# Hybrid encoder trunk, one core: sums of squares with tokens on partitions, and the condition ahead of the squares

## The chip, the cores and the metric

One Trainium2 chip; the kernel runs on one core. The metric is the device time of one execution in microseconds, 2192.99 us before the change: the median of three runs, 2190.62 to 2194.06. Everything is float32; large matmuls take their operands as pairs of rounded parts, hi and lo, and run three products.

## The reference

Two layers over 256 tokens of width 2048. Each layer is modulated by a condition vector and has two groups of attention heads side by side, then an MLP with squared ReLU:

```
cond = silu(c)
for l in range(2):
    mod = cond @ w_ada[l] + b_ada[l]            # six vectors of 2048
    h = rmsnorm(x) * (1 + sc_a) + sh_a
    proj = h @ w_in[l]                          # dq, dk, dv, cq, ckv, kr
    out_a = diff_attention(dq, dk, dv, positions, bias_table, lam)
    q = rmsnorm(cq, q_norm_g[l]) @ w_uq[l]
    kv = rmsnorm(ckv, kv_norm_g[l]) @ w_ukv[l]
    out_b = mla_attention(q, kv, rope(kr))
    x = x + g_a * (concat(out_a, out_b) @ w_o[l])
    h = rmsnorm(x) * (1 + sc_m) + sh_m
    x = x + g_m * (square(relu(h @ w_mlp_in[l])) @ w_mlp_out[l])
return rmsnorm(x, final_norm_g)
```

where `rmsnorm(x) = x * rsqrt(mean(x*x, -1) + 1e-6) * g`. The change concerns `cond` and all these norms but the last.

## The kernel before

The residual `x` is kept transposed: features on the 128 partitions, 16 blocks of 256 tokens in the free dimension. A norm therefore needs sums across partitions. It squares `x` on ScalarE, adds blocks on VectorE where it can, and multiplies by a 128x128 matrix of constants 1/n (`mean`) on TensorE (`rstd`, L536). Each column of the product is one token's mean, repeated on all 128 partitions. `root` (L542, L543) takes the square root on ScalarE and the reciprocal on VectorE, both of 128x256. The result `rstd` multiplies rows of `x` directly, in `modulated` (`ht`, L620), `latent` (`lt`, L645) and `scaled` (L610).

There are eight such norms: the first, in `setup`, directly over `x`; in each layer the two latent norms (`ckv`, then `cq`); that of layer 0's MLP; and those behind `ahead_rest`, for layer 1's input and layer 1's MLP, where the matmuls start on unnormalised `x` and the norm comes in later. The final norm has its own code and is not touched.

The modulation vectors are products of `cond` with 1 MB tiles of `w_ada`, on VectorE: one instruction of 128x2048 per tile (`ada`, L304), whose sum is one column of `macc`. `cond` is made in `setup`: one row of 2048 is multiplied by a row of `mean` in four `pc` matmuls (L357), which spreads it over 128 partitions, and ScalarE applies Silu (L358). Between two parts of layer 0's input projection (`by_k`, `pk`), four tiles are summed for the next two blocks of `x`; the first `ht` needs four. SyncE issues nearly all loads in program order. The tiles of `w_ada` and the split weights share five buffers (`raw`), so a load waits until VectorE has released the buffer it takes.

The instruction order on each engine is set by a scheduler that goes through the program in the order written, and by manual constraints (`follow`: the one instruction is issued behind the other, without a wait). Other small work lies between the parts of the first projection (`fills`): the relative bias, `lambdas` (`pl`, a matmul of 4 columns), the rope tables. `setup`, `bias_setup` and `distances` prepare that from `pos`, `K` (constants) and `vec` (small parameters).

Of the kernel before, what the change touches and what calls it, by code (L numbers as in the profile page):

```python
# [10 lines left out]
F32 = mybir.dt.float32  # L11
F32R = mybir.dt.float32r
I32 = mybir.dt.int32
AF = mybir.ActivationFunctionType
# [3 lines left out]
P = 128  # L18
T = 256
TX = T + 2  # L20
D = 2048
NK = D // P
# [5 lines left out]
EPS = 1e-6  # L28
# [75 lines left out]
class Trunk:  # L104
# [230 lines left out]
    def setup(self):  # L335
        nc, io, cp = self.nc, self.io, self.cp
        self.ada_plan()
        self.cond = cp.tile([P, D], F32, name="cond")
        row = self.wp.tile([1, D], F32, tag="raw", name="c_row", bufs=5)
        nc.sync.dma_start(row, io["c"])  # L340
        self.pos = cp.tile([P, T + 8], I32, name="pos")
        nc.scalar.dma_start(self.pos, io["pos"])
        self.K = cp.tile([P, NCONST], F32, name="K")
        nc.scalar.dma_start(self.K, io["consts"])
        self.vec = cp.tile([P, NVEC], F32, name="vec")
        nc.scalar.dma_start(self.vec, io["vec"])
        self.x = cp.tile([P, NK, T], F32, name="x")
        for q in range(4):
            nc.sync.dma_start(self.x[:, 4 * q : 4 * q + 4], io["xT"][:, 4 * q : 4 * q + 4])
        self.mean = {}  # L350
        for n in (D, 2 * P):
            self.mean[n] = cp.tile([P, P], F32, name=f"mean{n}")
            nc.gpsimd.memset(self.mean[n], 1.0 / n)
        for j in range(4):
            c = slice(512 * j, 512 * j + 512)
            ps = self.bank("pc").rearrange("p a b -> p (a b)")
            nc.tensor.matmul(ps, self.mean[D][:1], row[:, c], start=True, stop=True)  # L357
            nc.scalar.activation(self.cond[:, c], ps, AF.Silu, scale=float(D))  # L358
        self.eps = cp.tile([P, 1], F32, name="eps")
        nc.gpsimd.memset(self.eps, EPS)  # L360
        self.ident = cp.tile([P, P], F32, name="ident")
        make_identity(nc, self.ident)
        self.bias_setup()
        self.rel = {0: self.distances(0)}
        ps = self.bank("pn")[:, 0]
        for k in range(0, NK, 2):
            t = self.t("sqx")
            last = nc.scalar.activation(t, self.x[:, k : k + 2], AF.Square)
            for i in range(2):
                nc.tensor.matmul(ps, self.mean[D], t[:, i], start=k + i == 0, stop=k + i == NK - 1)  # L370
        self.follow(nc.scalar.activation(self.s("warm", 1), self.eps, AF.Sqrt), last)
        return self.root(ps)

    def fills(self):
        m = {"l": self.lambdas, "r": self.rope_setup, "e": lambda: self.bias_out(self.last)}
# [23 lines left out]
    def bias_setup(self):  # L399
        nc, K, pos = self.nc, self.K, self.pos  # L400
        n = T + 8
        half = lambda s, dt=F32: self.up.tile([P, 2 * T], dt, tag="u", name=self.name(s))
        ih, il, fh, fl = (half(s, dt)[:, :n] for s, dt in (("ih", I32), ("il", I32), ("fh", F32), ("fl", F32)))
        nc.vector.tensor_scalar(ih, pos, 16, None, ALU.arith_shift_right)
        nc.vector.tensor_scalar(il, pos, 0xFFFF, None, ALU.bitwise_and)
        nc.vector.tensor_copy(fh, ih)
        nc.vector.tensor_copy(fl, il)
        lh, ll = [], []
        for i in range(2):
            lsc = half("lsc")  # L410
            trep = self.vec[:, V_T + 16 * i : V_T + 16 * i + 16].unsqueeze(2).broadcast_to([P, 16, 32])
            delta = K[:, C_DELTA : C_DELTA + 32].unsqueeze(1).broadcast_to([P, 16, 32])
            nc.vector.tensor_tensor(lsc.rearrange("p (a b) -> p a b", a=16), trep, delta, ALU.mult)
            lh.append(half("lsch", F32R))
            ll.append(half("lscl", F32R))
            nc.scalar.activation(lh[i], lsc, AF.Copy)
            nc.vector.tensor_tensor(ll[i], lsc, lh[i].bitcast(F32), ALU.subtract)
        self.bias = self.cp.tile([P, HD, 2, T], F32, name="bias")
        self.bt = fh, fl, lh, ll
# [109 lines left out]

    def rstd(self, acc, n):  # L530

        nc = self.nc
        ps = self.bank("pn")[:, 0]
        acc = acc[:2] + acc[3:]
        for i, a in enumerate(acc):
            nc.tensor.matmul(ps, self.mean[n], a, start=i == 0, stop=i == len(acc) - 1)  # L536
        return self.root(ps)

    def root(self, ps):
        nc = self.nc  # L540
        r = self.cp.tile([P, T], F32, tag="rstd", name=self.name("rstd"), bufs=2)
        nc.scalar.activation(r, ps, AF.Sqrt, bias=self.eps)  # L542
        nc.vector.reciprocal(r, r)  # L543
        return r

    def ahead(self, l, sh, sc, src):

# [35 lines left out]
    def ahead_rest(self, st, first, acc, after, loads=0):  # L583

        h = []
        for p in range(first, 8):
            if p >= loads:
                self.rate = RATE_K
            if p == after:
                r = self.rstd(acc, D)  # L590
            self.ahead_step(st, p)
            if p >= after:
                upto = 2 * (p - after + 1) if loads else NK * (p - after + 1) // (8 - after)
                if p == 7:
                    upto = NK
                while len(h) < upto:
                    h += self.modulated(
                        r, len(h), self.mod[st.l, st.sh], self.mod[st.l, st.sc], after=self.lo if loads else None
                    )
        st.r = r  # L600
        return h
# [28 lines left out]
            self.last = ins  # L630
        return out

    def latent(self, vals, g):

        nc = self.nc
        acc = None
        for v in vals:
            acc = self.sumsq(acc, v, scale=2.0 if len(vals) == 2 else 1.0)
        r = self.rstd(acc, D if len(vals) == 2 else 2 * P)
        out = []  # L640
        for b, v in enumerate(vals):
            t = self.t("lt")
            for i in range(2):
                k = 2 * b + i
                nc.vector.scalar_tensor_tensor(t[:, i], v[:, i], g[:, k : k + 1], r, ALU.mult, ALU.mult)  # L645
            out += self.split(t, "lat")
        return out
# [25 lines left out]
    def layer(self, l, acc, st):  # L673
# [34 lines left out]
        def keys():  # L708
            ps = self.bank("pkr")
            self.tile_cols(ps[:, 0], io["w_kr"][l], h)  # L710
            self.kr = self.rope_k(ps[:, 0])
# [38 lines left out]
        def probs(hd):  # L750
            return lambda: a.append(self.diff_probs(l, self.diff_scores(hd, q[hd], kk[hd])))
# [13 lines left out]
        if l == 0:  # L765
            next_by_k(range(done, 4))(h)
            q += [self.copy(ps, "q", qs) for ps in banks[3:]]
            ckv += self.latent([ckr], gkv)
            kk.append(self.copy(later[0], "k", -1.0))
            q.append(self.copy(later[1], "q", qs))  # L770
            keys()
            order = [(0, kk, -1.0), (2, kk, -1.0), (4, kk, -1.0)]
            for n, (i, dst, scale) in enumerate(order):
                col(i, dst, scale)()
                if n == 0:
                    cq += self.latent(cqr, gq)
                got = self.diff_scores(n, q[n], kk[n])
                col(i + 1, dst, scale)()
                a.append(self.diff_probs(l, got, self.copied if n == 2 else None))
        else:  # L780
            def two(i, dst, scale):
                ps = self.wides([io["w_q"][0, i + j] for j in range(2)], h)
                dst.append(self.joined(ps, self.u("qk"), scale))

            two(0, q, qs)
            two(8, kk, -1.0)
            ckv += self.latent([ckr], gkv)
            for hd in range(1, HD):
                two(2 * hd, q, qs)
                probs(hd - 1)()  # L790
                two(8 + 2 * hd, kk, -1.0)
                if hd == 1:
                    cq += self.latent(cqr, gq)
            keys()
            self.rate = RATE_A2
        up_k()
# [450 lines left out]
def _layout(i):  # L1247
# [4 lines left out]
    pos = f["positions"][0]  # L1252
    order = [j + 4 * t for j in range(4) for t in range(2)]
    posq = np.tile(pos.reshape(8, 32).T, (4, 1))[:, order]
    a["pos"] = np.ascontiguousarray(np.concatenate([np.broadcast_to(pos, (P, T)), posq], 1))
    a["consts"] = consts()
    feat = lambda v, n: v.reshape(n, P).T
    vec = [feat(f["b_ada"][l], 96) for l in range(2)]
    vec += [feat(f["diff_subln_g"][l], 2) for l in range(2)]
# [1 line left out]
    vec += [feat(f["kv_norm_g"][l], 2) for l in range(2)]  # L1261
    vec += [np.stack([f[f"diff_lambda_{a}{j}"][l] for a in "qk" for l in range(2) for j in (1, 2)], 1)]
    vec += [np.repeat(f["rel_bias_table"].reshape(8, 4, HD).transpose(1, 0, 2).reshape(4, 32), 32, 0)]
    a["vec"] = np.ascontiguousarray(np.concatenate(vec, 1))
    assert a["vec"].shape == (P, NVEC)
    a["fg"] = np.ascontiguousarray(np.broadcast_to(f["final_norm_g"], (P, D)))
    a["w_ada"] = np.ascontiguousarray(f["w_ada"].transpose(0, 2, 1)).reshape(2, 96, P, D)
    keep = {k: [] for k in ("w_a", "w_d", "w_t", "w_a1", "w_q", "w_kr", "w_dv", "w_uq", "w_uk", "w_uv", "w_oa", "w_ob", "w_m0", "w_n0", "w_m1", "w_m2")}
# [49 lines left out]
```

## Time and profile before

| what | value |
|---|---|
| median of three runs | 2192.99 us |
| the profiled execution | 2192.04 us |
| its span, first to last instruction | 2190.2 us |
| mean granted TensorE clock | 0.995 |
| TensorE busy | 2155.7 us, 98% |
| VectorE busy | 1620.7 us, 74% |
| ScalarE busy | 1153.3 us, 53% |
| mean DMA rate | 268 GB/s |

The median of the runs lies 0.95 us above the profiled execution. All rows below come from this one execution. PE is TensorE, PEld its weight load, DVE VectorE, ACT ScalarE, POOL GpSimd, SP SyncE. A matmul's listed duration contains its way through the array; how fast matmuls follow each other is read from their starts.

### The profile page before, as it was taken

Reading aid. Unit: us, or ns where it says so; the run is one execution under the profiler, and the core shown is the slowest. Engines: PE = TensorE matmul, PEld = TensorE weight load, DVE = VectorE, ACT = ScalarE, POOL = GpSimd, SP = SyncE. Lnnn points to the kernel's source line nnn. Section 1 sums busy time; section 2 is a strip of 40 time slices with the busy share of each in tenths; the row PEclk is TensorE's granted clock in tenths of the full one; section 3 lists DMA queues with packets and bytes.
Section 4 is the critical chain, followed back from the end, with each engine's and each line's share of the span. In section 5 each row is a group of like instructions: output and inputs, shape, how many; then the busy total and the mean of one; then the engine's idle time right before and its main releaser. Section 6 shows DMA issues by size and latency. Waiting matters only on the chain.

```text
span 2190.2 us, 30242 instructions
## 1 busy us (share of the span) xinstructions
PE 2155.7 (98%) x11938; PEld 1884.5 (86%) x11938; DVE 1620.7 (74%) x2162; ACT 1153.3 (53%) x1730; POOL 26.7 (1%) x43
## 2 busy tenths in 40 slices
PE   7999999999999999999999999999999999999998
PEld 5899889898888888888888888999888888888886
DVE  7989988988778778788799876798545545545566
ACT  6555664455455355355456555647546535534544
POOL 0000000000000000000001000000000000000000
PEclk9999999999999999999999999999999999999999
DMA  9986888799888888888868765686555555555552
GB/s 400 383 337 233 342 335 298 258 362 346 310 322 323 328 305 339 328 308 318 323 231 307 250 250 211 243 301 217 192 194 187 189 195 189 190 194 191 187 198 94
DMA packets 85826, 586.39 MB, mean 268 GB/s; under 512 B 9522, under 2 KB 9906, under 8 KB 19634
## 3 DMA queue, kind: packets, MB, share of 16 engines
q1 hardware_dynamic: 85106, 583.84, 72.6%
q8 instruction: 93, 1.52, 0.3%
q10 hardware_dynamic: 576, 0.62, 0.1%
q14 instruction: 51, 0.41, 0.0%
HBM read 582.32 MB, written 2.10 MB: 267 GB/s over the span
## 4 chain that ended last, share of the span: by engine, by line
PE 92%; DVE 6%; ACT 2%; DMA 1%; issue 0%; ACTq 0%; DVEq 0%; SPq 0%
PE ps L208 24%; PE ps L211 13%; PE py L1022 11%; PE py L1020 11%; PE py L1024 11%; DVE ada L304 3%; PE pk L189 2%; PE pk L188 2%; PE pk L187 2%; PE pv L258 2%; PE pv L260 2%; PE pv L259 2%; PE pk L244 1%; DVE lo L151 1%; PE pss L189 1%; PE pss L187 1%
## 5 line engine op out<-in xcount | busy, mean ns | idle before, releaser
L151 DVE TENSOR_TENSOR lo<-raw,hi 128x1024 fp32r<-128x1024 f32 (+1 forms) x720 | 849.2, 1195 | 463.5 <-ACT hi L148 294.6
L148 ACT ACTIVATE hi<-raw 128x1024 fp32r<-128x1024 f32 (+1 forms) x720 | 737.6, 1035 | 632.1 <-PE py L1024 360.4
L208 PE MATMUL ps<-h,hi 128*128 128x512 f32 x2016 | 472.1, 391 | 1.2 <-ACT hi L148 1.2
L208 PEld LDWEIGHTS ps<-h,hi 128*128 128x128 f32 x2016 | 374.9, 188 | 77.8 <-ACT hi L148 2.1
L304 DVE SCALAR_TENSOR_TENSOR ada<-ada,cond 128x2048 f32<-128x2048 f32 x192 | 437.4, 2285 | 1.4 <-ACT cond L358 1.1
L1020 PE MATMUL py<-hi,hid 128*128 128x512 f32 x1024 | 326.5, 390 | 0.0
L1022 PE MATMUL py<-lo,hid 128*128 128x512 f32 x1024 | 325.9, 389 | 0.0
L1024 PE MATMUL py<-hi,hid 128*128 128x512 f32 x1024 | 325.7, 389 | 0.0
L211 PEld LDWEIGHTS ps<-h,lo 128*128 128x128 f32 x2016 | 250.5, 192 | 5.0
L211 PE MATMUL ps<-h,lo 128*128 128x256 f32 x2016 | 252.0, 283 | 0.0
L1022 PEld LDWEIGHTS py<-lo,hid 128*128 128x128 f32 x1024 | 192.2, 188 | 40.2 <-DVE lo L151 0.4
L1024 PEld LDWEIGHTS py<-hi,hid 128*128 128x128 f32 x1024 | 192.2, 188 | 40.0
L1020 PEld LDWEIGHTS py<-hi,hid 128*128 128x128 f32 x1024 | 191.3, 188 | 38.8
L1059 ACT ACTIVATE sum<-ps 128x256 f32<-128x256 f32 x110 | 42.1, 383 | 128.3 <-PE ps L211 128.0
L187 PE MATMUL pk<-h,hi 128*128 128x256 f32 x304 | 86.4, 288 | 7.0 <-ACT hi L148 3.6
L189 PE MATMUL pk<-h,lo 128*128 128x256 f32 x304 | 86.7, 289 | 0.8 <-DVE lo L151 0.8
L188 PE MATMUL pk<-h,hi 128*128 128x256 f32 x304 | 87.1, 288 | 0.0
L181 DVE TENSOR_TENSOR hid<-relu,hid 128x256 fp32r<-128x256 f32 x128 | 48.3, 421 | 46.7 <-ACT hid L180 46.7
L244 PE MATMUL pk<-hf,w 128*128 128x256 f32 x288 | 66.1, 391 | 9.4 <-ACT hf L628 9.4
L244 PEld LDWEIGHTS pk<-hf,w 128*128 128x128 f32 x288 | 56.4, 197 | 18.3 <-ACT hf L628 10.1
L187 PEld LDWEIGHTS pk<-h,hi 128*128 128x128 f32 x304 | 58.9, 195 | 8.3 <-ACT hi L148 4.4
L623 ACT ACTIVATE h<-ht,mod 128x256 fp32r<-128x256 f32 x64 | 29.5, 500 | 59.4 <-DVE ht L620 59.2
(262 smaller groups left out, 2590.2 us busy)
## 6 DMA issues: line engine op xcount, KB each, us to landing
raw<-in_w_m SPq DMA_DIRECT2D x238, 1024.0 KB, 4.9
ada<-in_w_ada SPq DMA_DIRECT2D x192, 1024.0 KB, 5.0
raw<-in_w_ob SPq DMA_DIRECT2D x24, 1024.0 KB, 4.8
raw<-in_w_dv SPq DMA_DIRECT2D x16, 1024.0 KB, 5.1
raw<-in_w_q SPq DMA_DIRECT2D x16, 1024.0 KB, 5.5
raw<-in_w_n SPq DMA_DIRECT2D x16, 768.0 KB, 5.6
w<-in_w_a SPq DMA_DIRECT2D x24, 384.0 KB, 9.3
raw<-in_w_a SPq DMA_DIRECT2D x12, 768.0 KB, 6.4
```

What stands on the lines that cost most here:

```text
L148: ins = nc.scalar.activation(hi, v, AF.Copy)
L151: ins = nc.vector.tensor_tensor(lo, v, hi.bitcast(F32), ALU.subtract)
L187: mm(ps, hi, x[0], start=first, stop=False, skip_group_check=shared)
L188: mm(ps, hi, x[1], start=False, stop=False, skip_group_check=shared)
L189: mm(ps, lo, x[0], start=False, stop=last, skip_group_check=shared)
L208: mm(ps.rearrange("p a b -> p (a b)"), part(w, 0, k), both, start=k == 0, stop=False)
L211: mm(ps[:, 0], part(w, 1, k), x, start=False, stop=k == nk - 1)
L244: self.nc.tensor.matmul(ps, w[i][:, j * P : j * P + P], whole[i], start=first, stop=last, skip_group_check=True)
L304: ins = nc.vector.scalar_tensor_tensor(w, w, 1.0, self.cond, ALU.mult, ALU.mult, accum_out=acc[:, i : i + 1])
L1020: mm(o, xh[:, tok], hi[:, part[j]], start=start, stop=False)
L1022: mm(o, xh[:, tok], lo[:, part[j]], start=False, stop=False)
L1024: mm(o, xl[:, tok], hi[:, part[j]], start=False, stop=stop)
```

## The change

Each mean of squares is now computed with tokens on partitions. `sums` makes the square the loaded operand, 128 features x 128 tokens, and streams one column of `mean`, so that each 128 tokens give one column of the result. `root` then works on 128x2. `spread` turns the two columns back to rows: a column of `r`, repeated 128 times, is transposed by TensorE into the other half of the same PSUM bank, and ScalarE copies it to `rstd`. The latent norms and those of `ahead_rest` put other work between the two halves, `total` and `spread`.

In `setup` three loads (`pos`, `consts`, `vec`) become one (`tab`), a Silu of one column is issued first on ScalarE, and the squares and the Copy of `bias_setup` are constrained to stand behind the Silu of `cond`.

```diff
-        self.pos = cp.tile([P, T + 8], I32, name="pos")
-        nc.scalar.dma_start(self.pos, io["pos"])
-        self.K = cp.tile([P, NCONST], F32, name="K")
-        nc.scalar.dma_start(self.K, io["consts"])
-        self.vec = cp.tile([P, NVEC], F32, name="vec")
-        nc.scalar.dma_start(self.vec, io["vec"])
+        tab = cp.tile([P, T + 8 + NCONST + NVEC], F32, name="tab")
+        nc.scalar.dma_start(tab, io["tab"])
+        self.pos = tab[:, : T + 8].bitcast(I32)
+        self.K = tab[:, T + 8 : T + 8 + NCONST]
+        self.vec = tab[:, T + 8 + NCONST :]
...
+        self.lead = nc.scalar.activation(self.s("warm", 1), self.eps, AF.Silu)
+        leads = []
         for j in range(4):
             c = slice(512 * j, 512 * j + 512)
             ps = self.bank("pc").rearrange("p a b -> p (a b)")
             nc.tensor.matmul(ps, self.mean[D][:1], row[:, c], start=True, stop=True)
-            nc.scalar.activation(self.cond[:, c], ps, AF.Silu, scale=float(D))
...
-        self.bias_setup()
+            self.lead = nc.scalar.activation(self.cond[:, c], ps, AF.Silu, scale=float(D))
+            leads.append(self.lead)
+            if j == 0:
+                self.bias_setup()
         self.rel = {0: self.distances(0)}
-        ps = self.bank("pn")[:, 0]
+        ps = self.bank("pn")
         for k in range(0, NK, 2):
             t = self.t("sqx")
             last = nc.scalar.activation(t, self.x[:, k : k + 2], AF.Square)
+            self.follow(last, leads[min(3, 1 + k // 4)])
             for i in range(2):
-                nc.tensor.matmul(ps, self.mean[D], t[:, i], start=k + i == 0, stop=k + i == NK - 1)
+                self.sums(ps, t[:, i], D, k + i == 0, k + i == NK - 1)
         self.follow(nc.scalar.activation(self.s("warm", 1), self.eps, AF.Sqrt), last)
-        return self.root(ps)
+        return self.spread(*self.root(ps))
...
     def rstd(self, acc, n):
+        return self.spread(*self.total(acc, n))
...
+    def sums(self, ps, a, n, first, last):
+        for t in range(2):
+            self.nc.tensor.matmul(
+                ps[:, 0, t : t + 1], a[:, t * P : (t + 1) * P], self.mean[n][:, :1],
+                start=first and t == 0, stop=last, skip_group_check=True,
+            )
+
     def root(self, ps):
         nc = self.nc
-        r = self.cp.tile([P, T], F32, tag="rstd", name=self.name("rstd"), bufs=2)
-        nc.scalar.activation(r, ps, AF.Sqrt, bias=self.eps)
+        r = self.s("root")
+        nc.scalar.activation(r, ps[:, 0, :2], AF.Sqrt, bias=self.eps)
         nc.vector.reciprocal(r, r)
-        return r
+        return ps, r
+
+    def spread(self, ps, r):
+        for t in range(2):
+            self.nc.tensor.transpose(
+                ps[:, 1, t * P : (t + 1) * P], r[:, t : t + 1].broadcast_to([P, P]), self.ident
+            )
+        out = self.cp.tile([P, T], F32, tag="rstd", name=self.name("rstd"), bufs=2)
+        self.nc.scalar.activation(out, ps[:, 1], AF.Copy)
+        return out
```

VectorE, from the end of its setup work to the first `ht`. `macc` and `mod` are the sums and vectors of the modulation, `rel` belongs to the bias. Before:

```order
L432 TENSOR_SCALAR rel_161<-rel_161 128x512
L304 SCALAR_TENSOR_TENSOR ada_213,macc_80<-ada_213,cond 128x2048
L304 SCALAR_TENSOR_TENSOR ada_216,macc_80<-ada_216,cond 128x2048
L543 RECIPROCAL rstd_204<-rstd_204 128x256
L316 TENSOR_TENSOR mod_79<-macc_80,vec 128x2
L304 SCALAR_TENSOR_TENSOR ada_220,macc_82<-ada_220,cond 128x2048
L304 SCALAR_TENSOR_TENSOR ada_223,macc_82<-ada_223,cond 128x2048
L314 SCALAR_TENSOR_TENSOR mod_81<-macc_82,vec 128x2
L620 SCALAR_TENSOR_TENSOR ht_227<-x,mod_81,rstd_204 128x256 x2
```

The same place on VectorE in the changed kernel, up to the first `ht`:

```order
L436 TENSOR_SCALAR rel_159<-rel_159 128x512
L304 SCALAR_TENSOR_TENSOR ada_231,macc_80<-ada_231,cond 128x2048
L558 RECIPROCAL root_218<-root_218 128x2
L304 SCALAR_TENSOR_TENSOR ada_234,macc_80<-ada_234,cond 128x2048
L316 TENSOR_TENSOR mod_79<-macc_80,tab 128x2
L304 SCALAR_TENSOR_TENSOR ada_238,macc_82<-ada_238,cond 128x2048
L304 SCALAR_TENSOR_TENSOR ada_241,macc_82<-ada_241,cond 128x2048
L314 SCALAR_TENSOR_TENSOR mod_81<-macc_82,tab 128x2
L647 SCALAR_TENSOR_TENSOR ht_245<-x,mod_81,rstd_223 128x256 x2
```

The reciprocal is of 128x2, and it stands one ada sum earlier: three of the four come behind it.

ScalarE, from its first instruction that computes to the squares of the first norm. `lsch` is the Copy of `bias_setup`. Before:

```order
L416 ACT_TABLE_LOAD
L416 ACTIVATE lsch_150<-lsc_148 128x512
L368 ACTIVATE sqx_170<-x 128x512
L368 ACTIVATE sqx_174<-x 128x512
L358 ACT_TABLE_LOAD
L358 ACTIVATE cond<-pc_121 128x512
L416 ACTIVATE lsch_156<-lsc_154 128x512
L368 ACTIVATE sqx_178<-x 128x512
L368 ACTIVATE sqx_182<-x 128x512
L358 ACTIVATE cond<-pc_124 128x512
L358 ACTIVATE cond<-pc_127 128x512
```

The same place on ScalarE in the changed kernel:

```order
L357 ACT_TABLE_LOAD
L357 ACTIVATE warm_124<-eps 128x1
L363 ACTIVATE cond<-pc_126 128x512
L420 ACTIVATE lsch_139<-lsc_137 128x512
L363 ACTIVATE cond<-pc_150 128x512
L371 ACTIVATE sqx_168<-x 128x512
L420 ACTIVATE lsch_145<-lsc_143 128x512
L363 ACTIVATE cond<-pc_153 128x512
L363 ACTIVATE cond<-pc_156 128x512
L371 ACTIVATE sqx_174<-x 128x512
```

One table load and one square stand ahead of the last quarter of `cond`, where two loads and five squares did.

TensorE, the end of the first norm's sums and the start of the first projection. Before, each row is one square's two matmuls:

```order
L370 MATMUL pn_169<-sqx_190,mean_117 128x256 x2
L370 MATMUL pn_169<-sqx_194,mean_117 128x256 x2
L370 MATMUL pn_169<-sqx_198,mean_117 128x256 x2
L244 MATMUL pk_207<-hf_236,w_239 128x256 x2
L244 MATMUL pk_208<-hf_236,w_239 128x256 x2
```

The same place on TensorE in the changed kernel; the operand named first streams, the second is loaded:

```order
L549 MATMUL pn_167<-mean_113,sqx_198 128x1 x4
L549 MATMUL pn_167<-mean_113,sqx_204 128x1 x4
L549 MATMUL pn_167<-mean_113,sqx_210 128x1 x4
L564 MATMUL pn_167<-ident,root_218 128x128 x2
L244 MATMUL pk_225<-hf_254,w_257 128x256 x2
L244 MATMUL pk_226<-hf_254,w_257 128x256 x2
```

There are twice as many matmuls, of one column, and the two transposes stand ahead of the first `pk`.

## Rows read from the trace of the kernel before

**Rows 1.** The page, parts 1 and 4: busy times, and the chain by engine.

```profile
PE 2155.7 (98%) x11938; PEld 1884.5 (86%) x11938; DVE 1620.7 (74%) x2162; ACT 1153.3 (53%) x1730; POOL 26.7 (1%) x43
...
PE 92%; DVE 6%; ACT 2%; DMA 1%; issue 0%; ACTq 0%; DVEq 0%; SPq 0%
```

**Rows 2.** TensorE's waits, whole span: line and releaser, us in total, times, longest.

```profile
PE pk L244 <- ACT hf L628: 9.4, 1, 9.4
...
PE pk L187 <- ACT h L623: 3.4, 1, 3.4
...
PE pn L536 <- DVE acc L527: 1.1, 2, 0.6
PE pa L189 <- DVE lo L151: 0.9, 2, 0.5
```

**Rows 3.** Chain that ended last, 0 to 160 us: start, us, what.

```profile
15.97 4.51 DVE ada L304 x4
20.48 1.67 DVE rstd L543
22.16 4.43 DVE ada L304 x4
...
28.77 13.36 PE pk L244 x48
...
105.93 10.36 PE pk L244 x48
```

**Rows 4.** Timeline, 0 to 45 us: start, us, engine, line, what, idle before.

```profile
2.69 7.16 PE L357 MATMUL pc<-c_row,mean 1*128 1x512 f32 x8 [2.69 <-DMA c_row<-in_c]
...
15.33 0.61 ACT L358 ACTIVATE cond<-pc 128x512 f32<-128x512 f32 x1
...
26.89 0.88 DVE L620 SCALAR_TENSOR_TENSOR ht<-x,mod,rstd 128x256 f32<-128x256 f32 x2
```

**Rows 5.** Windows: us, busy of PE, PEld, DVE, ACT, POOL; clock, DMA share, GB/s.

```profile
27.00:30.00 3.00, 1.24 (x3) 1.06 (x4) 2.77 (x8) 2.59 (x6) 0.00 (x0) 0.50 1.01 426
...
33.00:36.00 3.00, 3.00 (x12) 2.52 (x12) 3.00 (x3) 2.96 (x5) 0.00 (x0) 0.78 1.05 420
410.00:415.00 5.00, 2.59 (x15) 2.59 (x16) 4.96 (x11) 2.14 (x5) 0.00 (x0) 0.82 0.35 140
```

**Rows 6.** Timeline, 41.98 to 42.1 us, weight loads.

```profile
41.96 0.19 PEld L385 LDWEIGHTS pl<-vec,mean 128*128 128x128 f32 x1
42.07 0.19 PEld L463 LDWEIGHTS pb<-oh,lsch 128*128 128x128 f32 x1
```

**Rows 7.** The tile pn: duration ns least, median, most; first and last start.

```profile
L370 PEld LDWEIGHTS pn<-sqx,mean x32: 186/190/337, 10.0 to 18.8; 128*128 128x128 f32 x32
```

**Rows 8.** Timeline, short windows on TensorE at 10, 11, 13 and 29 us.

```profile
10.02 0.80 PE L370 MATMUL pn<-sqx,mean 128*128 128x256 f32 x1 [0.17 <-ACT sqx L368]
...
10.02 1.65 PE L370 MATMUL pn<-sqx,mean 128*128 128x256 f32 x3 [0.17 <-ACT sqx L368]
...
12.32 1.06 PE L370 MATMUL pn<-sqx,mean 128*128 128x256 f32 x2
...
28.77 1.65 PE L244 MATMUL pk<-hf,w 128*128 128x256 f32 x3 [9.40 <-ACT hf L628]
```

**Rows 9.** Timeline, 0 to 45 and 150 to 185 us: small instructions.

```profile
18.80 0.20 ACT L371 ACTIVATE warm<-eps 128x1 f32<-128x1 f32 x1
...
179.94 0.16 DVE L1115 RECIPROCAL r<-tot 128x2 f32<-128x2 f32 x1
```

**Rows 10.** Chain that ended last, 1085 to 1095 us: sixteen transposes.

```profile
1090.30 1.75 PE yt L1033 x16
```

**Rows 11.** Chain that ended last, 398 to 425 us, layer 0's MLP norm.

```profile
409.03 0.48 ACT rstd L542
409.54 1.76 DVE rstd L543
...
413.64 0.21 PE pk L189
...
417.03 0.12 PE pk L187
```

More of the change, by code (lines that the diff above doesn't have):

```diff
@@ L353, in setup @@
             nc.gpsimd.memset(self.mean[n], 1.0 / n)
+        self.eps = cp.tile([P, 1], F32, name="eps")
+        nc.gpsimd.memset(self.eps, EPS)
+        self.ident = cp.tile([P, P], F32, name="ident")
+        make_identity(nc, self.ident)
+        self.lead = nc.scalar.activation(self.s("warm", 1), self.eps, AF.Silu)
+        leads = []
         for j in range(4):
@@ L357, in setup @@
             nc.tensor.matmul(ps, self.mean[D][:1], row[:, c], start=True, stop=True)
-            nc.scalar.activation(self.cond[:, c], ps, AF.Silu, scale=float(D))
[L359 to L362, printed above, removed]
-        self.bias_setup()
+            self.lead = nc.scalar.activation(self.cond[:, c], ps, AF.Silu, scale=float(D))
+            leads.append(self.lead)
+            if j == 0:
+                self.bias_setup()
         self.rel = {0: self.distances(0)}
-        ps = self.bank("pn")[:, 0]
+        ps = self.bank("pn")
         for k in range(0, NK, 2):
@@ L415, in bias_setup @@
             ll.append(half("lscl", F32R))
-            nc.scalar.activation(lh[i], lsc, AF.Copy)
+            self.follow(nc.scalar.activation(lh[i], lsc, AF.Copy), self.lead)
             nc.vector.tensor_tensor(ll[i], lsc, lh[i].bitcast(F32), ALU.subtract)
@@ L530, in rstd, with total @@
     def rstd(self, acc, n):
-        nc = self.nc
-        ps = self.bank("pn")[:, 0]
+        return self.spread(*self.total(acc, n))
+    def total(self, acc, n):
+        ps = self.bank("pn")
         acc = acc[:2] + acc[3:]
         for i, a in enumerate(acc):
-            nc.tensor.matmul(ps, self.mean[n], a, start=i == 0, stop=i == len(acc) - 1)
+            self.sums(ps, a, n, i == 0, i == len(acc) - 1)
         return self.root(ps)
+    def sums(self, ps, a, n, first, last):
[4 more added lines that the diff above has]
+            )
     def root(self, ps):
         nc = self.nc
-        r = self.cp.tile([P, T], F32, tag="rstd", name=self.name("rstd"), bufs=2)
-        nc.scalar.activation(r, ps, AF.Sqrt, bias=self.eps)
+        r = self.s("root")
+        nc.scalar.activation(r, ps[:, 0, :2], AF.Sqrt, bias=self.eps)
         nc.vector.reciprocal(r, r)
-        return r
+        return ps, r
[7 more added lines that the diff above has]
+        return out
     def ahead(self, l, sh, sc, src):
@@ L589, in ahead_rest @@
             if p == after:
-                r = self.rstd(acc, D)
+                r = self.total(acc, D)
             self.ahead_step(st, p)
+            if p == after:
+                r = self.spread(*r)
             if p >= after:
@@ L631, in modulated, with latent @@
         return out
-    def latent(self, vals, g):
-        nc = self.nc
+    def latent(self, vals):
         acc = None
@@ L638, in latent, with latent_rest @@
             acc = self.sumsq(acc, v, scale=2.0 if len(vals) == 2 else 1.0)
-        r = self.rstd(acc, D if len(vals) == 2 else 2 * P)
+        return vals, self.total(acc, D if len(vals) == 2 else 2 * P)
+    def latent_rest(self, st, g):
+        nc = self.nc
+        vals, r = st[0], self.spread(*st[1])
         out = []
@@ L767, in layer @@
             q += [self.copy(ps, "q", qs) for ps in banks[3:]]
-            ckv += self.latent([ckr], gkv)
+            lv = self.latent([ckr])
             kk.append(self.copy(later[0], "k", -1.0))
@@ L771, in layer @@
             keys()
+            ckv += self.latent_rest(lv, gkv)
             order = [(0, kk, -1.0), (2, kk, -1.0), (4, kk, -1.0)]
@@ L775, in layer @@
                 if n == 0:
-                    cq += self.latent(cqr, gq)
+                    lq = self.latent(cqr)
                 got = self.diff_scores(n, q[n], kk[n])
                 col(i + 1, dst, scale)()
+                if n == 0:
+                    cq += self.latent_rest(lq, gq)
                 a.append(self.diff_probs(l, got, self.copied if n == 2 else None))
@@ L786, in layer @@
             two(8, kk, -1.0)
-            ckv += self.latent([ckr], gkv)
+            lv = self.latent([ckr])
             for hd in range(1, HD):
                 two(2 * hd, q, qs)
+                if hd == 1:
+                    ckv += self.latent_rest(lv, gkv)
+                if hd == 2:
+                    cq += self.latent_rest(lq, gq)
                 probs(hd - 1)()
@@ L792, in layer @@
                 if hd == 1:
-                    cq += self.latent(cqr, gq)
+                    lq = self.latent(cqr)
             keys()
@@ L1254, in _layout @@
     posq = np.tile(pos.reshape(8, 32).T, (4, 1))[:, order]
-    a["pos"] = np.ascontiguousarray(np.concatenate([np.broadcast_to(pos, (P, T)), posq], 1))
-    a["consts"] = consts()
+    pos = np.ascontiguousarray(np.concatenate([np.broadcast_to(pos, (P, T)), posq], 1).astype(np.int32, copy=False))
     feat = lambda v, n: v.reshape(n, P).T
@@ L1263, in _layout @@
     vec += [np.repeat(f["rel_bias_table"].reshape(8, 4, HD).transpose(1, 0, 2).reshape(4, 32), 32, 0)]
-    a["vec"] = np.ascontiguousarray(np.concatenate(vec, 1))
-    assert a["vec"].shape == (P, NVEC)
+    a["tab"] = np.concatenate([pos.view(np.float32), consts()] + vec, 1)
+    assert a["tab"].shape == (P, T + 8 + NCONST + NVEC)
     a["fg"] = np.ascontiguousarray(np.broadcast_to(f["final_norm_g"], (P, D)))
```

## Prediction

> **What bounds the kernel now.** I read the page's totals first: TensorE is busy 98% of the span, and the chain that ended last lies on it for 92% [rows 1]. So a change that only shortens work on other engines is worth something only where TensorE stands still. The list of TensorE's waits over the whole span names those places: 9.4 us before the first `pk` matmul of layer 0, 3.4 us at the norm of layer 0's MLP, and about 1 us in all at each of two lines near the other norms, `pa` and `pn` [rows 2]. The first is by far the largest, so the chain of the first 160 us comes next: it runs through VectorE, two ada sums (4.51 us), the reciprocal (1.67), two more sums (4.43), and then the first `pk`, after which it keeps returning to VectorE's ada sums [rows 3]. The timeline shows why: the last quarter of `cond` is written at 15.33 to 15.94, the first ada sum starts at 15.97, and `ht` at 26.89 needs four such sums and the reciprocal [rows 3, 4]. From there to about 130 us VectorE, TensorE and the DMA queues are all near full (33 to 36 us: 3.00 of 3 us on two engines, 1.05 of DMA), with VectorE last [rows 5]. So what moves the first `ht` moves everything behind it by about as much, and I count it in full.
>
> **The change: the first us.** Three edits pull `cond` forward: one table load fewer ahead of it, Silu ahead of the squares, one load for the constants. The eight `pc` records run from 2.69 to 9.85 [rows 4], so the first quarter has been ready since about 4.5 us. Now ScalarE takes each quarter as it comes, and `cond` ends near 10.5. VectorE's own setup work then ends near 11.3, and the first ada sum runs from about 11.4 to 13.6 instead of 15.97 to 18.2. If nothing else changed, 4.5 us would be won.
>
> But VectorE's order has changed too: the reciprocal stands behind the first ada sum, where it stood behind the second. It waits for the new root, and the root for all sums of squares. Queued behind it on VectorE are three ada sums, `mod` and `ht`; behind those, on the load queue, the loads that reuse the ada tiles' buffers. So the question is when TensorE ends the sums. Before: 16 matmuls, 32 records of 256 columns. Now each square is the loaded operand and one column streams: 32 matmuls, hence 64 records, each with its own 128x128 weight load. One column streams in next to no time, so the spacing is that of weight loads.
>
> The trace has one such pair: `pl`, 4 columns, float32. Its second load starts at 41.96 and the load behind it at 42.07: 0.11 us apart [rows 6]. That is in a warm stretch. In the first us TensorE is not warm: the first `pn` records of 256 columns follow each other at 0.43 us (three take 1.65, one 0.80), twice the 0.216 us of the `pk` records of the same width at 105.93 (10.36 / 48). Three `pk` records at 28.77 take the same 1.65 us, and there the granted clock is 0.50, the 1.2 GHz level [rows 3, 5, 8]. So TensorE starts at that level, and is still at it at 12.32, where two records take 1.06; later in the same run the loads are short [rows 7, 8]. Single weight loads behave alike: 0.337 us at most and 0.190 in the median for `pn` [rows 7]. So I take twice 0.11, rounded to 0.215 us. Bounds: 0.11 (the `pl` pair) and 0.337 (the longest load, with nothing overlapped).
>
> Would the sums lift the clock? The eight `pc` matmuls, one row deep, ran 7.16 us without a gap and the next records were still at 0.43 us; under the `pn` records, 128 rows by 256 columns, it rose [rows 4, 7, 8]. The trace has no run of one-column matmuls; I take the low level for all 64.
>
> The sum: sums start when `pc` is out, 9.6; 64 x 0.215 = 13.8; 0.2 for the last to drain: 23.6. Root on 128x2: 0.20, as the warm activation of 128x1, with 0.05 for the hand-over; the reciprocal of 128x2 is 0.16 [rows 9]: 24.0. Then one ada sum more than before stands behind it, 2.21 (4.43 / 2): 26.2; and as before 4.75 from there to `ht` (22.15 to 26.89 [rows 3, 4]): 31.0 against 26.89, **+4.1 us**. The two transposes and the copy that make `rstd` lie beside those ada sums and are over by about 25.5. VectorE stands still for some 10 us, from 13.6 to 23.8. The DMA queues do not add to it: at the 426 GB/s of [rows 5], from 3 us on, the constants, x, the first four ada tiles and the first weights (8.2 MB together) are in by about 23.
>
> The Trainium skill (TensorE: Matmul & The Clock Gate, LDWEIGHTS) prices a load by its columns at one fixed rate, an estimate of 0.107 us for 128, at either clock level. The warm pair agrees; by that rule the 64 would take 6.8 us. The loads of 0.337 us in the slow stretch speak against a fixed rate [rows 7]. It is the second rival below.
>
> **The change: the other seven norms.** These run at the 2.4 GHz level. Per norm the sums cost TensorE the same: 8 loads x 0.11 = 0.88 against four records of 256 columns, 4 x 0.216 = 0.86 us [rows 3, 6]. New are two transposes, at 0.11 each (16 `yt` records in 1.75 us [rows 10]): 0.22 us. Layer 0's MLP norm is taken apart below; its transposes sit in an idle stretch. The other six are where TensorE is full, and I let one of them meet a wait: five times 0.22 is **+1.1 us**. What goes is 1.59 us of VectorE per norm (1.75 to 0.16), which pays only where TensorE waits for VectorE. The waits that could shrink are `pa` and `pn` of [rows 2], 0.9 + 1.1, both on VectorE. I take **-0.9**, of the 0 to -2.0 that they allow. The transposes of these norms stand some 30 to 65 TensorE rows behind their sums, 5 us or more, so a root held up on VectorE behind an ada sum has time to arrive.
>
> At layer 0's MLP norm all is in one line, and TensorE waits [rows 2, 11]. Before: root 0.48, reciprocal 1.76, then `ht` at 411.3. Now, from 409.03: root 0.20, hand-over, reciprocal 0.16, done 409.45; weight load, two transposes and drain 0.55; copy of 128x256 0.47 as the old root; `ht` near 410.65: **-0.65 us**. A by-product stays out of the sum: after that wait the granted clock averages 0.82 over 410 to 415 [rows 5], and for about 3.4 us the `pk` records follow at 0.21 instead of 0.12 [rows 11]. If the shorter wait spares that, another -1.6.
>
> Front +4.1, seven norms +1.1 - 0.9 - 0.65 = -0.45: **+3.65 us**. The profiled execution spans 2190.2 and took 2192.04 us; it becomes 2195.7. The median of the runs is 2192.99, 0.95 above it, so the forecast is 2196.6.
>
> **Rivals.** First, the clock does rise during the sums, as it did during the old `pn`. With 15 records slow until 12.75 us and 49 at 0.11, the sums end at 18.3, the reciprocal at 18.7, `ht` at 25.7: -1.2, with -0.45 2190.4 for the profiled execution, 2191.3 as a median. For it: the same engine did so at the same time before. Against: it did not under `pc`.
>
> Second, the not-slower side: weight loads keep 0.11 us whatever the clock. The squares then end the chain: last square on ScalarE near 14.5, sums near 16.8, reciprocal 17.2, `ht` 24.2: -2.7, with -0.45 a median of 2189.9. It decides as soon as the spacing is under 0.15 us: at 0.15 the sums end at 19.4, `ht` at 26.8, and the front is even.
>
> Third, much slower: load and matmul do not overlap with one column, 0.337 us each. 64 x 0.337 = 21.6, sums end at 31.4, reciprocal 31.8, `ht` 38.8: +11.9, with -0.45 2204.4. Against: the `pl` pair did overlap.
>
> **Numbers.** Forecast 0.58, first rival 0.17, second 0.13, third 0.12. 0.2% is 4.4 us, about the least that a measurement of this kernel can tell from no change. Within the forecast, +3.65 with 2 us either way, by the waits credited, the clock at the MLP norm and how fast the first `pk` warms up, 0.4 lies above 4.4: slower is 0.23 + 0.12, with a little for what I have not seen 0.37. Faster needs the second rival and the clock by-product together: 0.10. Same: 0.53. The range goes from just below the second rival, 2189.5, to 2202, which cuts most of the third off; the forecast's own is 2194.5 to 2198.5.
>
> **What would show it.** In the changed profile: the first ada sum near 11.4 us, then VectorE idle until the reciprocal near 23.8; `pn` weight loads 0.21 us apart from 9.6 to 23.5; first `ht` near 31.0, first `pk` near 32.9. If the loads are 0.11 us apart, the forecast is wrong and the first or second rival holds, by when they narrow. At the MLP norm the wait before `pk` should be near 2.7 us with the transposes inside it. If TensorE idles before a transpose at another norm, my +1.1 is too small.

## The result, and the profile after

The changed kernel takes 2200.68 us (median of 6 runs, 2199.42 to 2201.95) against 2192.18 for the kernel before (6 runs): ratio 1.0039, 95% interval 1.0026 to 1.0052. It is 8.5 us slower; the forecast was 2196.6, in the range 2189.5 to 2202. The result lies inside that range but above the band that the prediction gave for its own mechanism, 2194.5 to 2198.5. The profiled execution spans 2199.2 us, 9.0 more than before.

The page's totals and its chain by engine, as in [rows 1]:

```profile
PE 2165.4 (98%) x12018; PEld 1896.7 (86%) x12018; DVE 1609.0 (73%) x2162; ACT 1154.1 (52%) x1738; POOL 27.8 (1%) x43
...
PE 90%; DVE 6%; ACT 2%; issue 1%; DMA 1%; DVEq 0%; ACTq 0%
```

VectorE is busy 11.7 us less and TensorE, which sets the time, 9.7 us more. TensorE's waits over the whole span, as in [rows 2]:

```profile
PE pk L244 <- ACT hf L655: 8.2, 1, 8.2
...
PE pa L189 <- DVE lo L151: 1.8, 2, 0.9
PE pk L187 <- ACT h L650: 1.5, 1, 1.5
...
PE pn L564 <- DVE root L558: 1.2, 2, 0.6
```

The wait at `pa`, the matmuls that run ahead on unnormalised `x`, doubled (0.9 before): they wait for `lo`, the low part of a weight, which VectorE writes. The wait at `pn` for `acc` (1.1 before) did not shrink:

```profile
PE pn L549 <- DVE acc L531: 1.1, 2, 0.7
```

The two new waits before transposes (`pn` for `root`) lie at the first norm and at layer 0's MLP norm, where TensorE stood still before too (timeline):

```profile
24.45 0.66 PE L564 MATMUL pn<-ident,root 128*128 128x128 f32 x2 [0.64 <-DVE root L558]
...
415.75 0.43 PE L564 MATMUL pn<-ident,root 128*128 128x128 f32 x2 [0.55 <-DVE root L558]
```

At the six other norms TensorE does not wait before a transpose. The chain of the first 45 us (start, us, what) tells of the front; before it ran through VectorE [rows 3]:

```profile
2.90 7.16 PE pc L362 x8
10.06 13.76 PE pn L549 x64
...
23.84 0.27 ACT root L557
...
24.13 0.17 DVE root L558
24.30 2.21 DVE ada L304 x2
...
26.69 4.43 DVE ada L304 x4
...
31.41 0.49 DVE ht L647
...
33.29 11.74 PE pk L244 x42
```

64 one-column matmuls in 13.76 us, then root, reciprocal and three ada sums, and `ht` at 31.41 where it was at 26.89 [rows 4]. VectorE in that time (timeline):

```profile
12.56 2.29 DVE L304 SCALAR_TENSOR_TENSOR ada<-ada,cond 128x2048 f32<-128x2048 f32 x1 [2.27 <-DMA ada<-in_w_ada]
...
24.13 0.17 DVE L558 RECIPROCAL root<-root 128x2 f32<-128x2 f32 x1 [9.27 <-ACT root L557]
```

It stands still for 9.27 us in front of an instruction of 0.17 us. At layer 0's MLP norm the chain [rows 11] now reads:

```profile
414.14 1.07 PE pn L549 x8
415.23 0.27 ACT root L557
...
415.75 0.45 PE pn L564 x2
416.21 0.39 ACT rstd L568
416.63 0.50 DVE ht L647
417.15 0.52 ACT h L650
417.71 1.65 PE pk L187 x6
```

From the end of the sums to the first `pk` this takes 2.5 us instead of 3.4, as meant. But the stretch at the low clock behind it is longer, and so is one at 137 us, ahead of all seven later norms. Windows (columns as in [rows 5]):

```profile
137.00:144.00 7.00, 6.45 (x28) 6.15 (x29) 6.01 (x10) 4.01 (x6) 0.00 (x0) 0.51 0.97 359
417.00:421.00 4.00, 3.29 (x15) 3.29 (x16) 4.00 (x12) 2.26 (x5) 0.00 (x0) 0.51 0.36 139
421.00:425.00 4.00, 4.00 (x25) 4.00 (x24) 2.16 (x6) 1.65 (x3) 0.00 (x0) 0.64 0.00 0
```

and of the kernel before, at the earlier place:

```profile
130.00:140.00 10.00, 7.35 (x48) 6.85 (x47) 9.68 (x19) 5.12 (x7) 0.00 (x0) 0.83 0.96 383
```

The granted clock is at its 1.2 GHz level for 6.8 us from 137.2 and from 417.1; in the trace of before for 3.4 us at either place (from 133.3 and from 413.2). The same TensorE records, matched between the two traces, give the account of the 9.0 us (start in the changed kernel, how much later than before):

| at, us | later by, us | what lies between |
|---|---|---|
| 33.3 | 4.5 | the front |
| 143.6 | 5.5 | low clock for 6.8 us instead of 3.4, ahead of the latent norms |
| 194.0 | 6.3 | two latent norms |
| 417.7 | 5.3 | layer 0's MLP norm, shorter by 1.0 |
| 423.6 | 6.4 | low clock for 6.8 us instead of 3.4 |
| 482.4 | 7.3 | in three steps, at 443, 451 and 482, in `pk`; not followed up |
| 1162.5 | 7.9 | layer 1's input norm |
| 1498.8 | 8.7 | 0.7 at layer 1's MLP norm; 0.5 at its latent norms, which an earlier step of -0.6, at 1185, cancels in this pair |

### The profile page after: what moved, and what is told of

It reads as the page before. It is cut to its first block, busy times and chain, and to the rows that moved or that the text cites. A ratio compares the mean times of both kernels' runs of the same rounds, so it can differ in the third digit from the quotient of the medians.

```text
span 2199.2 us, 30404 instructions
## 1 busy us (share of the span) xinstructions
PE 2165.4 (98%) x12018; PEld 1896.7 (86%) x12018; DVE 1609.0 (73%) x2162; ACT 1154.1 (52%) x1738; POOL 27.8 (1%) x43
## 4 chain that ended last, share of the span: by engine, by line
PE 90%; DVE 6%; ACT 2%; issue 1%; DMA 1%; DVEq 0%; ACTq 0%
PE ps L208 24%; PE ps L211 13%; PE py L1060 11%; PE py L1062 11%; PE py L1058 11%; DVE ada L304 3%; PE pv L258 2%; PE pv L260 1%; PE pv L259 1%; PE pk L189 1%; PE pk L187 1%; PE pk L188 1%; DVE lo L151 1%; PE pk L244 1%; PE pn L549 1%
## 5 line engine op out<-in xcount | busy, mean ns | idle before, releaser
L189 PEld LDWEIGHTS pk<-h,lo 128*128 128x128 f32 x304 | 60.2, 199 | 1.7 <-DVE lo L151 1.6
```

What stands on the lines that cost most here:

```text
L189: mm(ps, lo, x[0], start=False, stop=last, skip_group_check=shared)
```

## The experiments

"Wide" is the form of before (256 columns, root and reciprocal of 128x256), "thin" that of the change. All are timed against the kernel before in five rounds (the added warm-up in three); its medians there are 2191.9 to 2192.2 us. The traces are of one execution each.

**Which part costs what.** Four runs. All eight norms wide, with only the edits of the first us kept:

```
-        return self.spread(*self.root(ps))        # setup, and so in total()
+        return self.wide_root(ps)                 # sqrt and reciprocal of 128x256
...
-    self.sums(ps, t[:, i], D, ...)
+    nc.tensor.matmul(ps, self.mean[D], t[:, i], ...)
```

Where later norms are wide, their two halves stand together again, as before the change.

> All eight norms as before the change (sums of 256 columns, root and reciprocal of 128x256), the edits of the first us kept. Theory (the late end of 64 one-column matmuls is what moved the first ht to 31.4): the squares are out at 14.3, the sums end between 16.5 and 19, the reciprocal stands behind the second ada sum and ht starts between 23.5 and 25.9, against 26.9 before and 31.4 changed; total 1 to 3.4 us below the kernel before. Rival (the new order of the first us is late by itself, through the ada loads or ScalarE): ht stays later than 29 and the total 2 to 4 us above before.

2191.45 us, ratio 1.0001 (0.9992 to 1.0010): no change. The late `ht` is gone, but less was won than the theory said. The sums ended at 20.4 and `ht` came at 27.42 in this execution (26.05 in the next run, same order): the 32 records of 256 columns stay at twice the time for longer than I allowed. Both the theory's size and the rival were off. The reciprocal stands behind two ada sums in these two runs, not behind one as in the changed kernel.

Only the first norm wide (the setup part of that diff):

> Only the first norm as before the change; the other seven with tokens on partitions. Theory (of the 8.5 us lost, 4.5 are the first norm and about 4 the seven norms, some 2.3 of these in two stretches of low clock): total 5.5 to 8 us below the changed kernel, so 0.6 to 3 us above the kernel before, and 3 to 4.5 us above the run with all norms wide. Rival (the seven norms cost nothing, as predicted with -0.45, and what came after the first norm is a consequence of the late start): 1.4 to 3.9 us below the kernel before and within 0.5 us of the run with all norms wide.

2193.63 us, 1.0007 (0.9998 to 1.0016): 7.1 us below the changed kernel. The seven norms cost 2193.63 - 2191.45 = 2.2 us, not nothing, and less than the 3 to 4.5 expected. The executions of the two runs overlap (2192.49 to 2194.51 against 2189.73 to 2193.21), so the size is rough.

Only the seven others wide (the `total` part of it):

> Only the first norm with tokens on partitions; the other seven as before the change. Theory: ht at 31.4 as in the changed kernel, total 4 to 5.5 us above the kernel before, and no second stretch of low clock longer than before at layer 0's MLP norm. Rival (the late start costs again further on): 8 to 9 us above the kernel before, as the changed kernel.

2196.79 us, 1.0020 (1.0011 to 1.0030): 4.8 us, with `ht` at 31.38. The front alone costs that, as the theory said. The seven norms behind a late front cost 2200.68 - 2196.79 = 3.9 us.

The changed kernel with the reciprocal behind four ada sums:

```
+        for g in (0, 1):
+            self.ada_need(0, g, 1)
...
-        return self.spread(*self.root(ps))
+        return self.spread(*self.root(ps, self.ada_last))   # follow(reciprocal, last ada sum)
```

> The changed kernel with the reciprocal of the first norm issued behind four ada sums on VectorE instead of behind one. Theory (VectorE stood idle in front of the reciprocal with ada sums queued behind it): the sums still end at 23.7, the transposes follow at 24.4, ht starts between 25.4 and 26, 5.4 to 6 us earlier than in the changed kernel; total 2 to 3.5 us above the kernel before. Rival (the ada sums would not have come earlier, for their loads or buffers): ht after 29, total within 2 us of the changed kernel.

2193.54 us, 1.0008 (0.9999 to 1.0016), 7.1 us below the changed kernel by moving one instruction of 0.17 us. VectorE's timeline:

```profile
17.23 2.29 DVE L304 SCALAR_TENSOR_TENSOR ada<-ada,cond 128x2048 f32<-128x2048 f32 x1
...
19.66 2.29 DVE L304 SCALAR_TENSOR_TENSOR ada<-ada,cond 128x2048 f32<-128x2048 f32 x1
...
24.12 0.17 DVE L561 RECIPROCAL root<-root 128x2 f32<-128x2 f32 x1 [2.15 <-ACT root L560]
...
25.54 0.88 DVE L652 SCALAR_TENSOR_TENSOR ht<-x,mod,rstd 128x256 f32<-128x256 f32 x2 [1.20 <-ACT rstd L573]
```

The sums end where they did, but the ada sums now run during them and `ht` starts at 25.54, as the theory said. The total is 1.5 us above the kernel before, less than the 2 to 3.5 expected. So the loss in front is the long sums together with the place of the reciprocal: without the long sums, or with the reciprocal last, it is gone. Short sums with the reciprocal behind one ada sum were not run.

**What spaces the one-column matmuls.** The changed kernel with a warm-up ahead of the sums:

```
+        for _ in range(5):
+            nc.tensor.matmul(junk, self.mean[D], first, start=True, stop=True)   # 128x512, unused
```

> The changed kernel with five 128x512 matmuls added on TensorE between pc and the sums of the first norm (nothing of them is used); the reciprocal stands behind the second ada sum here. Theory (the spacing of the one-column matmuls follows the clock): while the clock is low they follow at 0.21 us, and once these added matmuls have raised it at 0.11 us, so the 64 take about 7 us instead of 13.8. Rival (0.21 us belongs to one-column matmuls with a load each, at any clock): 13.8 us again, and the sums end about 4 us later than 23.7.

2199.42 us, 1.0033 (1.0021 to 1.0045). TensorE's timeline and its windows:

```profile
10.08 6.86 PE L372 MATMUL pw<-x,mean 128*128 128x512 f32 x10
16.78 9.27 PE L554 MATMUL pn<-mean,sqx 128*128 128x1 f32 x64
```

```profile
18.00:20.00 2.00, 2.00 (x20) 2.00 (x19) 0.00 (x0) 1.71 (x3) 0.00 (x0) 1.00 0.98 398
20.00:22.00 2.00, 2.00 (x18) 2.00 (x17) 0.00 (x0) 0.86 (x2) 0.00 (x0) 0.90 1.03 416
22.00:24.00 2.00, 2.00 (x12) 2.00 (x11) 0.00 (x0) 0.00 (x0) 0.00 (x0) 0.50 1.08 452
24.00:26.00 2.00, 2.00 (x10) 1.97 (x10) 0.00 (x0) 0.00 (x0) 0.00 (x0) 0.50 1.00 422
```

One run shows both levels: the starts of the first 44 are 0.112 us apart, and at 21.6 us, while TensorE does nothing but one-column matmuls, the granted clock falls to 0.50 and the rest are 0.213 us apart, as all 64 in the changed kernel. The theory holds for the spacing, not for the sum: the 64 take 9.3 us, not 7, since they do not hold the clock up in this execution. The first rival of the prediction (the sums themselves lift it) was refuted already by the changed kernel, whose 64 all stay 0.213 us apart; the second (0.11 us at any clock) falls with both. The Trainium skill (TensorE: Matmul & The Clock Gate, LDWEIGHTS) gives loads one rate, an estimate of 0.107 us for 128 columns. The high level agrees with its 0.112; at the low level the measured 0.213 us decides against it.

**What the seven norms cost.** The run with only the first norm wide, its transposes behind `ahead_rest` issued earlier:

```
             for j, ps in enumerate(st.banks):
                 self.mac(...)
...
+            if mid is not None and i == 0:
+                mid()                  # spread, after 18 pa matmuls instead of 36
```

> The run with only the first norm wide, with the transposes of the two norms behind ahead_rest issued 18 pa matmuls behind the sums instead of 36. Theory (these two norms cost 0.5 us each because rstd now waits for transposes that stand 36 matmuls, 4.4 us, behind the sums, so VectorE starts its ht 2.3 us later and its lo comes late for pa): ht of layer 1's input norm starts some 2 us earlier, the wait of pa for lo falls from 1.8 to about 0.9 us in all, total 0.7 to 1.2 us below that run. Rival (the wait is set by the ada sum that stands before lo on VectorE): the wait stays at 1.8 us and the total within 0.3 us.

2192.30 us, 1.0002 (0.9993 to 1.0010): 1.3 us below that run, with intervals that overlap, so the traces have to carry the reading. Where `rstd` and `ht` of layer 1's input norm start, on ScalarE and VectorE (timeline); first all norms wide:

```profile
1136.74 0.45 ACT L564 ACTIVATE rstd<-pn,eps 128x256 f32<-128x256 f32 x1
...
1140.25 0.88 DVE L656 SCALAR_TENSOR_TENSOR ht<-x,mod,rstd 128x256 f32<-128x256 f32 x2
```

the first norm wide, the others thin:

```profile
1136.85 0.26 ACT L557 ACTIVATE root<-pn,eps 128x2 f32<-128x2 f32 x1 [0.22 <-PE pn L549]
...
1142.03 0.36 ACT L575 ACTIVATE rstd<-pn 128x256 f32<-128x256 f32 x1
1142.57 1.27 DVE L654 SCALAR_TENSOR_TENSOR ht<-x,mod,rstd 128x256 f32<-128x256 f32 x3
```

and with the transposes early:

```profile
1138.53 0.36 ACT L575 ACTIVATE rstd<-pn 128x256 f32<-128x256 f32 x1
...
1139.53 1.27 DVE L658 SCALAR_TENSOR_TENSOR ht<-x,mod,rstd 128x256 f32<-128x256 f32 x3
```

In the second the reciprocal is done at 1137.4, but `rstd` waits for transposes that stand 36 `pa` matmuls behind the sums; VectorE starts `ht` 2.3 us later than with wide norms (1.8 later counted from the start of the sums, which stand 0.5 us later there), and its `lo` comes late. With the transposes early, `ht` starts 5.0 us behind the start of the sums, as with wide norms. The wait of `pa` for `lo`, with the transposes late and early:

```profile
PE pa L189 <- DVE lo L151: 1.8, 2, 0.9
...
PE pa L189 <- DVE lo L151: 0.2, 1, 0.2
```

Against the same records TensorE gains 0.5 us at layer 1's input norm and 0.7 at its MLP norm. The theory holds.

Then the low clock at layer 0's MLP norm, with four unused 128x256 matmuls added there to the run with only the first norm wide:

```
+        self.nc.tensor.matmul(ps[:, 1], self.mean[n], self.x[:, 0], ...)   # before the transposes
         out = self.spread(ps, r)
+        for _ in range(3):
+            self.nc.tensor.matmul(ps[:, 0], self.mean[n], self.x[:, 0], ...)
```

> The run with only the first norm wide, with four added 128x256 matmuls at layer 0's MLP norm, one between the sums and the transposes and three behind the transposes (work added, nothing of it is used). Theory (with one-column sums in place of those of 256 columns TensorE does less around this wait, and so is held at the low level for 6.8 us instead of 3.4): the stretch of low clock falls to 3.4 us or none, total 1 to 2 us below that run. Rival (the length of the stretch is chance or follows the wait alone): 6.8 us of low clock again, total within 0.5 us or above.

2193.53 us, 1.0005 (0.9996 to 1.0014): no gain, 6.8 us of low clock from 408.0, and the added matmuls run in it. They also put the first `pk` 2.3 us further behind the sums, so the time by itself says little. Windows:

```profile
406.00:409.00 3.00, 2.27 (x14) 1.95 (x14) 1.51 (x4) 1.23 (x4) 0.00 (x0) 0.83 0.41 119
409.00:413.00 4.00, 3.53 (x10) 2.45 (x9) 2.78 (x7) 1.74 (x4) 0.00 (x0) 0.50 0.39 157
413.00:417.00 4.00, 4.00 (x28) 4.00 (x27) 2.12 (x7) 1.85 (x4) 0.00 (x0) 0.77 0.02 4
```

The theory fell.

**A version that beats both.** All norms wide, and the reciprocal behind the four ada sums (the two diffs above together):

> All norms as before the change, the edits of the first us kept, and the reciprocal of the first norm issued behind four ada sums. Theory (with the sums out of the way the four ada sums set the first ht): sums end between 19 and 20.4, the ada sums at 21.9, the reciprocal ends at 23.7, ht starts near 24, 2.9 us earlier than before; total 2 to 3.5 us below the kernel before. Rival (what is won in front is lost again before 140 us, since the weights and the ada loads do not come earlier): first pk near 26, but the pk records at 135 us no earlier than 0.7 us before their old time, total within 1 us of the kernel before.

2189.54 us, 0.9986 (0.9977 to 0.9995): 2.6 us below the kernel before, as the theory said. VectorE's timeline:

```profile
19.45 2.29 DVE L304 SCALAR_TENSOR_TENSOR ada<-ada,cond 128x2048 f32<-128x2048 f32 x1
...
21.67 1.75 DVE L568 RECIPROCAL rstd<-rstd 128x256 f32<-128x256 f32 x1
...
23.55 0.88 DVE L661 SCALAR_TENSOR_TENSOR ht<-x,mod,rstd 128x256 f32<-128x256 f32 x2
```

No idle before the reciprocal, `ht` 3.3 us earlier than before. TensorE leads the kernel before by about 4.4 us until 128 us, but of that 1.6 is left at the end of this execution: 1.1 goes with a stretch of low clock at 128 us (6.8 us instead of 3.4), the rest later. Also, a wide norm at layer 0's MLP has 6.8 us of low clock here, so that length does not follow the form of the norm alone.

On top of it, thin norms where they should pay, by a second `thin()` beside `total()` and a call of it at that norm:

> The run with all norms wide and the reciprocal last in front, and of the seven other norms only that of layer 0's MLP with tokens on partitions. Theory (this norm saves 1.0 us in its chain, and the runs with one-column sums there were at low clock for 6.8 us behind it): the wait before pk falls from 3.4 to about 2.4 us or 1.5 behind the transposes; low clock of 6.8 us gives about 1 back, so the total lies within 1 us of the run without it. Rival (the length of the low clock there is chance): the average of many executions lies 1 us below the run without it.

2188.51 us, 0.9984 (0.9975 to 0.9993). The wait before `pk` is 1.5 us behind the transposes, and this execution had 3.4 us of low clock, with thin sums.

> The run with all norms wide and the reciprocal last in front, and of the seven other norms only the two behind ahead_rest with tokens on partitions, their transposes 18 matmuls behind the sums. Theory (with the transposes early, VectorE's relief is worth what the transposes cost, or a little more): no wait of pa for lo above 0.9 us in all, total within 0.7 us of the run without it, below rather than above. Rival (the transposes and the sums cost TensorE 0.3 us per norm whatever stands around them): 0.6 us above.

2188.89 us, 0.9983 (0.9974 to 0.9992); the wait for `lo` is 0.2 us.

> Both together: three norms with tokens on partitions (layer 0's MLP, and the two behind ahead_rest with early transposes), the first norm and the four latent norms wide, the reciprocal last in front. Theory: total 0 to 1.5 us below the run with all norms wide and the reciprocal last, so 2.6 to 4 us below the kernel before. Rival (one-column sums let the clock fall and give the gain back): at or above that run.

2189.31 us, 0.9988 (0.9979 to 0.9997). The three lie 0.2 to 1.0 us below the run they build on, their intervals overlap its own, and both together give no more than either: a gain from thin norms on top is not shown. That all four beat the kernel before is.

> All norms wide and the reciprocal last in front, but for the four latent norms, which are as in the changed kernel: tokens on partitions, their transposes 28 to 65 TensorE rows behind the sums. Theory (the latent norms are where the seven norms' price lies, since TensorE is full there and VectorE's relief buys nothing): 0.5 us per layer, total 0.7 to 1.8 us above the run with all norms wide and the reciprocal last. Rival (the price of the seven norms lies with the two norms behind ahead_rest and their late transposes alone): within 0.4 us of that run.

2189.78 us, 0.9997 (0.9987 to 1.0006), its executions from 2187.96 to 2196.25: too wide apart to price 1 us. In its trace TensorE falls back by 0.6 us against the run without at each layer's latent norms, that is 0.3 per norm where the prediction had 0.22. By time it stays open.

## Why the prediction was right, and where it was not

The sum was right in sign and 4.85 us short (8.5 against 3.65): 0.4 of it in the front, the rest behind it.

**The front: right in mechanism and size.** Forecast: `pn` records 0.215 us apart from 9.6 to 23.6, reciprocal at 24.0, `ht` at 31.0, +4.1. Measured: 0.213 us, 10.0 to 23.8, 24.13, 31.41, +4.5; of the 0.4 between, 0.2 is `c_row` landing later (`pc` starts at 2.90 instead of 2.69). It also reached TensorE in full, as the prediction counted it: its records are 4.4 us late up to 130 us. The choice that carried it was to take the spacing of loads at the low level as twice that of the `pl` pair [rows 6], and to count the ada sums queued behind the waiting reciprocal. A miss without effect: the first ada sum starts at 12.56, not 11.4, since its tile lands then; VectorE idles after it anyway. The timed run of the front alone gives 4.8.

**The seven norms: the term that failed, -0.45 against 3.9 measured.** Its parts:
- Transposes, +1.1: right in kind and somewhat small. TensorE falls back by 0.2 to 0.3 us at each of the six norms (0.2 at layer 1's input norm, 0.5 to 0.6 per layer for the latent norms), some 1.6 in all.
- VectorE's relief, -0.9 out of the waits of [rows 2]: wrong in sign. The step that failed is crediting VectorE's 1.59 us per norm against the waits at `pa` and `pn`, with 0 as the worst case. The wait at `pn` stayed at 1.1 us and that at `pa` grew from 0.9 to 1.8. The 31 to 64 TensorE rows between sums and transposes let the root arrive in time, as the prediction said: TensorE idles before no transpose at these six norms, so the sign that it named for too small a +1.1 did not show. But the prediction left out that `rstd`, and VectorE's `ht` and `lo` behind it, now wait through those rows (36 at the norms behind `ahead_rest`). The early transposes show it: with them the wait at `pa` is 0.2 us.
- MLP norm, -0.65: measured -1.0 at its first `pk`, right in sign.
- The clock by-product, kept out of the sum with -1.6: in the profiled execution it went the other way, about +1.1 us at 420. As much again went at 138 us, where no norm stands: TensorE waits 2.4 us for `hi` there in both traces, and the sums of the first of the seven norms come at 161 us. That stretch is no part of the seven norms' own price, though it is in the 9.0 of the profiled execution.

**What stays open: the low clock.** Over all executions timed, the mean clock gives 16.9 us at the low level in the changed kernel and 12.7 with the seven norms wide, 23.5 and 21.1 in the pair with a wide first norm (one less the granted clock, listed to 0.001, times twice the span; mean over the executions). The measure is coarse: single executions of the changed kernel give 13 to 22 us. The low level takes about twice the time (0.213 against 0.112 us for a load), so half of these differences, 2.1 and 1.2 us, is what the clock can explain of the 3.9 and 2.2. What sets the length at the MLP norm isn't settled: in the profiles it was 6.8 us in seven of eight kernels with that norm thin, and 3.4 in four of six with it wide. Added matmuls did not shorten it, and each form has shown either length. The stretch at 128 to 138 us, ahead of these norms, varies as well: none in three of the fourteen kernels, 3.4 us in seven and 6.8 in four. So how much of the 3.9 and 2.2 is the norms' doing through the clock, and how much is chance, is not shown.

## What to carry to other kernels

Price a matmul of one column by its weight load, at the clock of the place where it runs, and do not expect a run of such matmuls to raise or hold that clock: 64 of them did neither here. Before shortening an instruction, look at where it stands in its engine's queue: moving a 0.17 us reciprocal behind the work that did not need it was worth 7 us here, while shortening seven others from 1.75 to 0.16 us gained nothing that the total shows. If a result has to pass through a second engine's queue (here transposes on TensorE), its latency is that queue's length at the place where they are written.

## What the runs showed of the hardware

A TensorE shown 100% busy is no sign of the clock: with the added 128x512 matmuls the records came to full speed (0.853 us apart at first, 0.430 from 14.8 us on), and under the one-column matmuls behind them the granted clock fell again, to 0.50, with TensorE busy throughout. And where no lower value has been recorded yet, the profile prints 1.00: in the first us of the changed kernel the windows say 1.00 while the loads follow at the low level's 0.213 us, so the spacing of records has to be read there, not the printed clock:

```profile
12.00:15.00 3.00, 3.00 (x16) 3.00 (x15) 2.30 (x2) 2.98 (x6) 0.00 (x0) 1.00 1.02 431
```
